# Sixty-four prompt tokens moved from a dense expert pass to a row-by-row one

## The chip, the cores and the metric

The kernel runs on one core of one Trainium2 chip. The metric is the device time of one launch in microseconds, as a median of runs. TensorE (PE) multiplies matrices, VectorE (DVE), ScalarE (ACT) and GpSimd (POOL) do the elementwise work, GpSimd also issues the indirect DMAs that gather rows, and SyncE (SP) issues all other DMAs.

## The reference

One transformer layer is computed for 1024 prompt tokens and for 32 sample tokens (8 sequences of 4). A projection feeds a state-space mixer and a windowed attention, both are joined by an output projection and a layer norm, and then comes a feed-forward part in which every token chooses 8 heads x 16 of 16384 experts. Only this last part is touched by the change:

```python
def block(xb):                      # xb: tokens x 1024, after the first layer norm
    qh = jnp.einsum('td,de->te', xb, w_q).reshape(-1, PEER_HEADS, PEER_DKEY)
    ...                             # top 16 of 128 keys on two sides, top 16 of their 256 sums
    e = ...                         # 128 expert numbers for each token
    g = jax.nn.softmax(sc.astype(F32), axis=-1)
    hid = jax.nn.gelu(jnp.einsum('thkd,td->thk', u_tab[e], xb).astype(F32), approximate=False)
    return jnp.einsum('thk,thkd->td', (g * hid).astype(xb.dtype), v_tab[e])
```

The result goes through `layer_norm(ALPHA * h + peer_ffn(h, ...))`. The tables `u_tab` and `v_tab` hold 16384 rows of 1024 floats (64 MB each).

## The kernel before, in words

**Two parts.** `PARTS` cuts the prompt into tokens 0 to 511, which go with the 32 sample tokens, and tokens 512 to 1023. `part(0)` and `part(1)` run `first` (projections, attention), `second` (scan, gates) and `third` (output projection, first norm), and `route` scores the keys and takes the top 16s on VectorE. Matrices are multiplied in three products of rounded parts (`hh`/`hl`, `whi`/`wlo`): each weight block `wraw` of 256 KB comes by a DMA of SP, ScalarE rounds it to `whi` (L366), and GpSimd or VectorE takes the rest `wlo` (L367). One weight block of 1024 x 128 is a step: 8 x 3 matmuls for each piece of its token columns, all at L425.

**Two ways through the experts.** The first way goes row by row (`gathers`). For 128 tokens at a time and for each of their 128 choices, one indirect DMA (L1823) fetches 128 rows of `u`, 512 KB, and VectorE multiplies and sums them against the token (L1849); then the same with 128 rows of `v`, which VectorE adds with weights (L1854). That is one row step for each (table, choice). The second way is dense (`dense`): for a set of tokens every one of the 16384 experts is computed, `gelu(u x)` times a table `g` that holds the token's gate or zero, and then `v` times that. There are 16 chunks of 1024 experts; a chunk is 8 steps over `u` (`hidden`) and 8 steps over `v` (`output`), 256 steps in all.

**Who goes which way.** `EXTRA = 64` splits the first part: tokens 0 to 447 (`TG`) go by row, tokens 448 to 511 are dense. The row plan has three tiles of 128 tokens with 2 x 128 row steps each, and a tile of 64 tokens whose choices are folded in two halves over the 128 partitions (`halfe`, `halfg`), with 2 x 64 row steps: 896 row steps. Dense are the 512 tokens of the second part, the 64 and the 32 sample tokens: `TE` = 608 columns, in the pieces `TPC` of 320 and 288.

**What sets the order.** The program is written out by generators ("lanes"). A step of matmuls is cut into ticks; at each tick the lanes advance by their rate, and what they emit stands there in every engine's queue. The row steps are such a lane, `pumping`. It starts in part 1 once `chooses` has the first tile's experts, at the rates `GATHER`, stands still at the end of `third`, runs at 0.2 per tick while the dense tables are made, and in the main loop at

```python
self.pumping.rate = self.left / ((len(steps) - 8) * DTICKS - 20)
```

so that what is left of the plan is spread over the 248 steps behind the first 8, with `DTICKS` = 4 ticks each. `ROWS` = 6 row buffers and `LOOK` = 5 mean that a row is fetched five row steps ahead, and a fetch waits until VectorE has used the buffer's last row. All queues are in order: on GpSimd the fetches stand between the casts `wlo`, on VectorE the row steps stand between `weigh` (L1671), `low` (L1677) and the sums of `output` (L1695).

**The tables.** Before the main loop `gates` makes the dense table in groups of 4 tokens: VectorE compares (`oo`, L1602), GpSimd weighs (L1604), TensorE multiplies (L1611), ScalarE stores to `gst` (L1621), and 32 tokens at a time go to DRAM (`gd`, 2 MB). The groups come in the order sample tokens, then the 64, then the four tiles of part 1: 152 groups. For the first two the experts were chosen earlier (`given = 2`); for the four tiles `choose` runs between the groups. Six steps over `u` run meanwhile, with `EARLY` ticks. The main loop reads the table back as `g`, 2.5 MB for each chunk.

Of the kernel before, what the change touches and what calls it, by code (L numbers as in the profile page):

```python
# [19 lines left out]
NB = 8  # L20
# [60 lines left out]
TICKS, ETICKS = [[6, 4, 4, 4], [5, 4, 4, 4]], 6  # L81
GATHER = [2.5, 3.2, 3, 0.0, 0.2]
DTICKS = 4
CACHE, SAMPLE, TOPS, TOPS2, CHOOSE = 0.1, 1.4, 1, 0.6, 1

START, LO1, LO2, LO3, LO4, LO5 = "vp", ["vvp", "vpp"], ["vp", "vp"], ["vp", "vp"], ["p", "p"], "vpppppp"
# [51 lines left out]
def layout(inp):  # L138
# [62 lines left out]
    "y": (TG, D),  # L201
# [12 lines left out]
def unlayout(r):  # L214
    y = r["y"]
    y1 = r["y1"].transpose(2, 1, 0).reshape(TE, D)
    yp = np.concatenate([y, y1[PD:PD + EXTRA], y1[:PD]])
# [6 lines left out]
    def cache(old, new):  # L224
# [3 lines left out]
        yp[None], y1[PD + EXTRA:].reshape(NB, NL, D),  # L228
# [23 lines left out]
class Build:  # L252
# [40 lines left out]
    def run(self):  # L293
# [16 lines left out]
        self.half_e = cp.tile([128, 64], I32, name="halfe")  # L310
        self.half_g = cp.tile([128, 64], F32, name="halfg")
# [3 lines left out]
        self.hx = dpool.tile([128, 8, NX], F32, name="hx")  # L315
# [3 lines left out]
        self.pumping, self.seat = None, None  # L319
# [9 lines left out]
    def start(self):  # L329
# [157 lines left out]
    def part(self, hf):  # L487
# [9 lines left out]
        if self.smp:  # L497
            xp = self.open("smp", side="right")
# [10 lines left out]
    def first(self, hf):  # L509
        two = len(self.pcs) == 2  # L510
        self.ring = [0, 1, 2] if two else [0, 1]
        self.ms, self.pvz = (4, 5) if two else (2, 3)
        self.sc = [self.bank(6), self.bank(7)] if two else [self.bank(4, 2), self.bank(6, 2)]
# [80 lines left out]
    def keyrows(self, ap, pr, ps):  # L594
# [11 lines left out]
        if not self.last:  # L606
            nc.sync.dma_start(self.kd[self.hf][:, pr], kk[:, :PT])
        if self.smp:
            nc.gpsimd.tensor_copy(self.sample[1][:, pr], kk[:, PT:])
        self.ready[pr] += 1  # L610

    def values(self, ap, pr, ps):
# [11 lines left out]
        for a in range(0, len(self.tiles), 4):  # L624
            tl = self.tiles[a:a + 4]
# [482 lines left out]
    def gated(self, zp, ps, k):  # L1108
# [23 lines left out]
        if k % 3 == 2:  # L1132
            yield

            while k < 11 and self.at < 3:
# [14 lines left out]
    def third(self, hf):  # L1150
# [82 lines left out]
        for i, (s, n) in enumerate(cuts):  # L1233
            for j, (k, h) in enumerate(END):
                self.step(self.parted(self.h), [acc[k][i]], [(s, n)], ETICKS, False, True, order=[4, 5, 6, 7, 0, 1, 2, 3], q=q0 + j,
# [11 lines left out]
        for i, (s, n) in enumerate(cuts):  # L1247
            while norms[i].live:
                norms[i].run()
            self.step(self.x, [out[i] if np_ == 2 else out[0][:, s:s + n]], [(s, n)], 4, q=q0, ahead=i == 0)  # L1250
        self.close(f"z{hf}", f"y{hf}", f"att{hf}", f"x{hf}")
        if not self.last:
# [3 lines left out]
            nc.sync.dma_start(self.hx, self.r[:, :, self.PT - EXTRA:])  # L1256
        else:
            sp = self.open(f"n{hf}", side="right")
            hx = sp.tile([128, 8, NX], F32, name="hx", tag="hx", bufs=1)
# [90 lines left out]
    def route(self, hf, first):  # L1350
# [10 lines left out]
        self.routed = self.tiles[:n], self.best  # L1361
        if self.last:
            others = [self.lane(self.experts(sp, *v)) for v in zip(((self.smp_e, self.smp_g), (self.ecol[-1], self.gate[-1])), (NS, 128), self.given)]
        else:
            self.gp = self.open("g")
# [533 lines left out]
```

## Time and profile before

| what | value |
|---|---|
| median of 3 runs | 3781.95 us (3780.59 to 3783.11) |
| the profiled execution's own time | 3779.82 us |
| its span, first to last instruction | 3778.1 us |
| mean granted TensorE clock | 0.959 |
| busy share of the span: PE, DVE, POOL, ACT | 92%, 71%, 63%, 34% |
| moved by DMA | 875.33 MB, mean 232 GB/s |

Spans below are in microseconds from the first instruction. The stages are: both parts up to 1760, the tables from 1760 to 2050, a turn into the main loop to 2090, the main loop to 3738, and the last norm. The granted clock is given as a share of full speed (1.00 is 2.4 GHz). The DMA share is the mean busy share of the core's 16 DMA engines; q0 carries the gathered rows, q1 everything that SP issues. A matmul's duration overlaps the next one's, so its cost is read from the distance of starts.

### The profile page before, as it was taken

The page shows a single profiled execution, that of the slowest core. Times are in us where ns is not written, and L with a number is a line of the kernel's source. Part 1 is how long each engine was busy: PE and PEld are TensorE (multiplying, and loading weights), DVE is VectorE, ACT ScalarE, POOL GpSimd, SP SyncE. Part 2 cuts the span into 40 slices and gives each one's busy share as a digit, 9 for nine tenths or more (in the row PEclk, how much of TensorE's full clock was granted, in tenths as well). Part 3 has the DMA queues.
Part 4 walks back from the last instruction along what each step waited for, and adds up shares of the span by engine and source line. Part 5 has one row for each costly group of instructions (what it writes and reads, how often), then busy time and mean ns, then how long its engine had stood idle before and what let it go on. Part 6 is the DMA issues. An engine that isn't in the chain of part 4 may idle for free.

```text
span 3778.1 us, 61732 instructions
## 1 busy us (share of the span) xinstructions
PE 3475.6 (92%) x22691; PEld 3142.5 (83%) x22691; DVE 2684.3 (71%) x5449; ACT 1285.9 (34%) x2347; POOL 2370.2 (63%) x2235
## 2 busy tenths in 40 slices
PE   8999998997998787996778999999999999999998
PEld 7757777986666565775668999999999999999997
DVE  2335655379768988889998967677767667776775
ACT  3423224252443334242556222222232222223222
POOL 3303555344656678734787877777778777777774
PEclk9999999998999898987898999999999999999999
DMA  5352235752446557811557889999999999999993
GB/s 166 116 164 85 84 103 182 252 178 79 141 141 226 169 161 235 300 58 65 186 196 283 319 317 355 329 322 313 325 319 365 327 329 334 319 315 322 327 328 132
DMA packets 386959, 875.33 MB, mean 232 GB/s; under 512 B 40416, under 2 KB 151392, under 8 KB 383712
## 3 DMA queue, kind: packets, MB, share of 16 engines
q0 software_dynamic: 129024, 469.82, 34.9%
q1 hardware_dynamic: 257632, 401.57, 32.0%
q8 instruction: 178, 2.92, 0.3%
q14 instruction: 125, 1.02, 0.1%
HBM read 805.34 MB, written 94.65 MB: 238 GB/s over the span
## 4 chain that ended last, share of the span: by engine, by line
PE 45%; DVE 8%; issue 4%; POOL 3%; DMA 2%; ACT 1%; DVEq 0%; POOLq 0%; SPq 0%; ACTq 0%
PE P L425 38%; PE P L1745 5%; DVE oo L1602 2%; POOL oo L1604 1%; DMA row<-in_v,ecol 1%; PE P L1611 1%; DVE P L1854 1%; POOL row L1823 1%; POOL wlo L367 1%; DVE mr L1341 0%; POOL eq L1542 0%; PE P L1275 0%; DMA lng<-in_ln 0%; DVE keys L1345 0%; DVE keys L1339 0%
## 5 line engine op out<-in xcount | busy, mean ns | idle before, releaser
L367 POOL TENSOR_TENSOR wlo<-wraw,whi 128x512 fp32r<-128x512 f32 (+1 forms) x621 | 807.0, 1305 | 604.0 <-ACT whi L366 548.7
L366 ACT ACTIVATE whi<-wraw 128x512 fp32r<-128x512 f32 (+1 forms) x820 | 499.9, 625 | 1390.8 <-PE P L425 583.0
L425 PE MATMUL P<-hh,whi 128*128 128x320 f32 (+3 forms) x2648 | 654.6, 312 | 7.5 <-ACT hh L1304 4.6
L425 PE MATMUL P<-hl,whi 128*128 128x320 f32 (+3 forms) x2648 | 653.6, 311 | 3.5 <-POOL hl L1296 3.2
L425 PE MATMUL P<-hh,wlo 128*128 128x320 f32 (+3 forms) x2648 | 647.7, 310 | 4.8 <-POOL wlo L367 4.5
L1854 DVE SCALAR_TENSOR_TENSOR P<-row,hid,P 128x1024 f32<-128x1024 f32 x448 | 575.3, 1284 | 28.7 <-DMA row<-in_v,ecol 14.7
L1849 DVE SCALAR_TENSOR_TENSOR row<-row,P 128x1024 f32<-128x1024 f32 x403 | 478.4, 1213 | 62.8 <-DMA row<-in_u,ecol 25.9
L1823 POOL DMA_INDIRECT row<-in_u,ecol x384 | 389.1, 1013 | 155.4 <-DVE row L1849 79.4
L425 PE MATMUL P<-xh,whi 128*128 128x272 f32 (+4 forms) x1288 | 434.6, 347 | 37.2 <-ACT xh L366 15.7
L425 PEld LDWEIGHTS P<-hh,whi 128*128 128x128 f32 x2648 | 445.2, 191 | 17.5 <-ACT hh L1304 5.0
L425 PEld LDWEIGHTS P<-hl,whi 128*128 128x128 f32 x2648 | 445.2, 191 | 13.1 <-POOL hl L1296 4.7
L425 PEld LDWEIGHTS P<-hh,wlo 128*128 128x128 f32 x2648 | 444.8, 191 | 13.1 <-POOL wlo L367 4.7
L1823 POOL DMA_INDIRECT row<-in_v,ecol x384 | 378.7, 986 | 101.7 <-issue 49.2
L425 PE MATMUL P<-xl,whi 128*128 128x272 f32 (+4 forms) x1288 | 421.9, 338 | 7.8 <-POOL xl L367 6.1
L425 PE MATMUL P<-xh,wlo 128*128 128x272 f32 (+4 forms) x1288 | 418.2, 335 | 0.0
L367 DVE TENSOR_TENSOR wlo<-wraw,whi 128x512 fp32r<-128x512 f32 (+1 forms) x199 | 212.6, 1069 | 211.1 <-ACT whi L366 202.3
L425 PE MATMUL P<-ah,wlo 128*128 128x320 f32 (+1 forms) x1536 | 341.3, 301 | 4.5 <-POOL wlo L367 4.5
L425 PE MATMUL P<-ah,whi 128*128 128x320 f32 (+1 forms) x1536 | 342.1, 302 | 0.0
L425 PE MATMUL P<-al,whi 128*128 128x320 f32 (+1 forms) x1536 | 340.8, 301 | 0.0
L425 PEld LDWEIGHTS P<-xh,whi 128*128 128x128 f32 (+1 forms) x1288 | 247.8, 196 | 69.8 <-ACT xh L366 17.0
L425 PEld LDWEIGHTS P<-xl,whi 128*128 128x128 f32 (+1 forms) x1288 | 247.6, 196 | 35.0 <-POOL xl L367 8.2
L425 PEld LDWEIGHTS P<-xh,wlo 128*128 128x128 f32 (+1 forms) x1288 | 247.2, 196 | 25.4 <-issue 4.2
(386 smaller groups left out, 6147.9 us busy)
## 6 DMA issues: line engine op xcount, KB each, us to landing
wraw<-in_ut SPq DMA_DIRECT2D x256, 256.0 KB, 6.0
wraw<-in_vd SPq DMA_DIRECT2D x256, 256.0 KB, 4.8
wraw<-in_wt SPq DMA_DIRECT2D x176, 256.0 KB, 2.9
gd<-gst SPq DMA_DIRECT2D x19, 2048.0 KB, 7.3
g<-gd SPq DMA_DIRECT2D x90, 320.0 KB, 9.8
wraw<-in_wo SPq DMA_DIRECT2D x64, 256.0 KB, 3.8
wraw<-in_wq SPq DMA_DIRECT2D x64, 256.0 KB, 3.0
out_sk<-in_ck SPq DMA_DIRECT2D x8, 2040.0 KB, 10.9
```

Of the source, the lines that this page charges most:

```text
L366: nc.scalar.activation(hi, src, AF.Copy)
L367: (eng or nc.vector).tensor_tensor(lo, src, hi.bitcast(F32), op=ALU.subtract)
L425: nc.tensor.matmul(outs[i], w[a][:, k, :m], x[b][k][:, s:s + n], start=first and st, stop=last and sp)
L1602: nc.vector.tensor_tensor(oo, iota.unsqueeze(1).unsqueeze(1).to_broadcast([128, 2, 4, 128]), eT[:, 0:2, t0:t0 + 4].unsqueeze(3).to_broadca ...
L1604: nc.gpsimd.tensor_tensor(oo[:, 1], oo[:, 1], eT[:, 2, t0:t0 + 4].unsqueeze(2).to_broadcast([128, 4, 128]), op=ALU.mult)
L1611: nc.tensor.matmul(gp[:, k * 128:(k + 1) * 128], oo[:, 1, k], oo[:, 0, k], start=True, stop=True)
L1745: nc.tensor.matmul(outs[i][j], self.ws[q0 + i][wi][:, e, :], x[xi][e][:, s:s + m], start=e == p == 0, stop=e == last and p == 2)
L1823: nc.gpsimd.indirect_dma_start(out=rows[k], out_offset=None, in_=t["uv"[tab]], in_offset=bass.IndirectOffsetOnAxis(ap=tables(gi)[0][:, s:s ...
L1849: nc.vector.scalar_tensor_tensor(r, r, 1.0, at, op0=ALU.mult, op1=ALU.mult, accum_out=hid[:, s:s + 1])
L1854: nc.vector.scalar_tensor_tensor(at, r, hid[:, s:s + 1], at, op0=ALU.mult, op1=ALU.add)
```

## The change

`EXTRA`, `TG`, `NX`, `halfe` and `halfg` go. All 512 tokens of the first part go by row: four tiles of 128, 4 x 2 x 128 = 1024 row steps. Dense are the 512 tokens of part 1 and the 32 samples: `TE` = 544 columns, `TPC` = 288 and 256, 17 table blocks of 32 tokens where there were 19, 136 groups where there were 152. `given` becomes 1, and while the tables' first tile has its experts chosen, the lane first waits for the top 16s of part 1 to be finished. `fetch` now asks whether a tile's experts are chosen (`self.chosen`). Several constants become lists by part with the same values for these two parts (`GATHER`, `TICKS`, `ETICKS`, `TOPS`, `SCORES`), and some conditions are written for more than two parts; those leave these two parts' instructions as they were. Rates of the row lane in part 1 and beside the tables are the same, so the same number of row steps is done before the main loop, and what is added falls into it.

```diff
 PARTS = [(0, 512, True), (512, 512, False)]
-EXTRA = 64
 TD, PD = PARTS[-1][:2]
-TG = TD - EXTRA
-NX = EXTRA + NS
-TE = PD + NX
+TE = PD + NS
...
-GATHER = [2.5, 3.2, 3, 0.0, 0.2]
+GATHER, GATHERT = [[0, 0, 0, 0], [2.5, 3.2, 3, 0.0]], 0.2
...
 def chooses
-            if s + m > TG:
-                for src, dst in ((e, self.half_e), (g, self.half_g)):
-                    for k in range(2):
-                        self.nc.sync.dma_start(dst[64 * k:64 * k + 64], src[:64, 64 * k:64 * k + 64])
-            if i == 0:
+            self.chosen += 1
+            if not self.pumping:
                 self.pumping = self.lane(self.gen, self.rate)
...
 def gates
-        work = [(NS, PD + EXTRA, 0), (EXTRA, PD, 128 - EXTRA)] + [(m, s, 0) for s, m in tiles]
-        given = 2
+        work = [(NS, PD)] + list((m, s) for s, m in tiles)
+        given = 1
...
-            if t0 == work[w][2] and 0 < w < len(work) - 1:
+            if t0 == 0 and w < len(work) - 1:
                 gen = experts(w + 1)
             next(gen, 0)
-            if t0 == work[w][2] + work[w][0] - 4 * OBUFS:
+            if t0 == work[w][0] - 4 * OBUFS:
+                while w < given and self.top.live:
+                    yield
                 for _ in gen:
                     pass
...
 def gathers
-        plan = [(gi, tab, s) for gi in range(NTG) for tab in range(2) for s in range(min(128, TG - gi * 128))]
-        self.left = len(plan)
+        plan = [(gi, tab, k) for gi in range(NTG) for tab in range(2) for k in range(128)]
+        self.left, ahead = len(plan), [0]
...
-                if s == m - 1:
+                if s == 127:
                     acc = seat(gp.tile([128, D], F32, name="acc", tag="acc"), at) if moved else at
-                    if m < 128:
-                        up = gp.tile([128, D], F32, name="up", tag="gh")
-                        nc.sync.dma_start(up[:m], acc[m:])
-                        nc.vector.tensor_tensor(acc[:m], acc[:m], up[:m], op=ALU.add)
-                    self.norm2(acc[:m], t["y"][gi * 128:gi * 128 + m], m)
+                    self.norm2(acc, t["y"][gi * 128:gi * 128 + 128], 128)
```

On TensorE, from the first dense step on, a product of one `k` stands in two pieces. Before:

```order
L425 MATMUL P<-hh,whi 128x320
L425 MATMUL P<-hh,whi 128x288
L425 MATMUL P<-hl,whi 128x320
L425 MATMUL P<-hl,whi 128x288
L425 MATMUL P<-hh,wlo 128x320
L425 MATMUL P<-hh,wlo 128x288
```

Now:

```order
L423 MATMUL P<-hh,whi 128x288
L423 MATMUL P<-hh,whi 128x256
L423 MATMUL P<-hl,whi 128x288
L423 MATMUL P<-hl,whi 128x256
L423 MATMUL P<-hh,wlo 128x288
L423 MATMUL P<-hh,wlo 128x256
```

Both pieces are narrower by 32 columns; the number of matmuls of a step stays 48.

On GpSimd, in the main loop where two `v` steps run as one double step, row fetches (DMA `row`) stand between casts (`wlo`). Before:

```order
L367 TENSOR_TENSOR wlo_20898<-wraw_20753,whi_20897 128x512
L1823 DMA row_20921<-in_u,ecol1_75 128x1024
L367 TENSOR_TENSOR wlo_20898<-wraw_20789,whi_20897 128x512
L1823 DMA row_20953<-in_u,ecol1_75 128x1024
L1823 DMA row_20968<-in_u,ecol1_75 128x1024
L1823 DMA row_20995<-in_u,ecol1_75 128x1024
L1823 DMA row_21010<-in_u,ecol1_75 128x1024
L367 TENSOR_TENSOR wlo_21019<-wraw_20826,whi_21018 128x512
```

Now:

```order
L365 TENSOR_TENSOR wlo_19669<-wraw_19521,whi_19668 128x512
L1821 DMA row_19692<-in_u,ecol1_75 128x1024
L365 TENSOR_TENSOR wlo_19669<-wraw_19557,whi_19668 128x512
L1821 DMA row_19712<-in_u,ecol1_75 128x1024
L1821 DMA row_19727<-in_u,ecol1_75 128x1024
L1821 DMA row_19754<-in_u,ecol1_75 128x1024
L1821 DMA row_19769<-in_u,ecol1_75 128x1024
L1821 DMA row_19784<-in_u,ecol1_75 128x1024
L365 TENSOR_TENSOR wlo_19793<-wraw_19597,whi_19792 128x512
```

Five fetches stand in a row where four stood: the row lane's rate is higher, and the casts are as many as before.

On VectorE, in the tables, the choice of the first tile's experts (`eq`, `ef`, `ei`) stood between compares of groups (`oo`) and row steps. Before:

```order
L1540 TENSOR_TENSOR eq_15670<-sf_15634,cf_15633 128x1024
L1602 TENSOR_TENSOR oo_15672<-P_64,eT1_13982 128x1024
L1854 SCALAR_TENSOR_TENSOR P_64<-row_13641,hid_9238,P_64 128x1024
L1602 TENSOR_TENSOR oo_15687<-P_64,eT1_13982 128x1024
L1602 TENSOR_TENSOR oo_15698<-P_64,eT1_13982 128x1024
L1545 TENSOR_REDUCE ef_15669<-eq_15670 128x64
L1602 TENSOR_TENSOR oo_15710<-P_64,eT1_13982 128x1024
L1540 TENSOR_TENSOR eq_15721<-sf_15634,cf_15633 128x1024
L1602 TENSOR_TENSOR oo_15723<-P_64,eT1_13982 128x1024
```

Now:

```order
L1542 TENSOR_TENSOR eq_15574<-sf_15566,cf_15565 128x1024
L1547 TENSOR_REDUCE ef_15573<-eq_15574 128x64
L1542 TENSOR_TENSOR eq_15578<-sf_15566,cf_15565 128x1024
L1547 TENSOR_REDUCE ef_15573<-eq_15578 128x64
L1549 CAST ei_15563<-ef_15573 128x128
L1558 TENSOR_SCALAR ej_15584<-ei_15563 128x128
L1559 TENSOR_SCALAR ej_15584<-ei_15563 128x128
L1561 CAST en_15585<-ej_15584 128x256
L1604 TENSOR_TENSOR oo_15593<-P_64,eT_13975 128x1024
```

Nothing stands between its steps any more: the compares that stood there are those of the 64 tokens, which are gone, and the row step there comes later.

## Rows read from the trace of the kernel before

**Rows 1.** Busy time by stage; columns in the second line, last two DMA share and rate.

```profile
core 0: us, PE busy (x) PEld busy (x) DVE busy (x) ACT busy (x) POOL busy (x), PEclk, DMA share, GB/s
0.00:1760.00 1760.00, 1557.40 (x9145) 1248.29 (x9145) 1177.19 (x3529) 634.23 (x1373) 885.99 (x888) 0.94 0.47 154
1760.00:2050.00 290.00, 221.01 (x1503) 205.18 (x1504) 275.11 (x389) 172.00 (x176) 229.12 (x213) 0.88 0.54 196
2050.00:2090.00 40.00, 32.00 (x204) 29.80 (x204) 24.52 (x23) 12.71 (x21) 20.85 (x17) 0.91 0.75 242
2090.00:3738.00 1648.00, 1638.99 (x11715) 1638.26 (x11714) 1186.25 (x1477) 453.18 (x753) 1230.21 (x1117) 1.00 0.92 324
3738.00:3778.00 40.00, 26.20 (x130) 20.99 (x128) 21.28 (x35) 13.81 (x26) 4.01 (x3) 0.83 0.18 63
```

**Rows 2.** What TensorE waited for in the main loop: us, times, longest.

```profile
PE P L425 <- POOL wlo L367: 9.0, 3, 4.5
```

**Rows 3.** TensorE's timeline in the main loop: start us, us, pieces of 320 and 288 columns.

```profile
2500.22 0.44 PE L425 MATMUL P<-hh,wlo 128*128 128x320 f32 x2
...
2502.74 0.44 PE L425 MATMUL P<-hh,wlo 128*128 128x320 f32 x2
```

**Rows 4.** TensorE's timeline in the first part's projections: 272 columns each.

```profile
158.34 0.29 PE L425 MATMUL P<-xh,whi 128*128 128x272 f32 x1
...
160.10 0.29 PE L425 MATMUL P<-xh,wlo 128*128 128x272 f32 x1
```

**Rows 5.** The DMA queues and issues of the main loop, 2090 to 3738 us.

```profile
DMA packets 245605, 534.47 MB, mean 324 GB/s; under 512 B 20965, under 2 KB 93413, under 8 KB 245462
q0 software_dynamic: 99040, 360.62, 60.3%
q1 hardware_dynamic: 146422, 171.91, 31.7%
g<-gd SPq DMA_DIRECT2D x90, 320.0 KB, 9.8
g<-gd SPq DMA_DIRECT2D x29, 256.0 KB, 8.6
```

**Rows 6.** Queues over 100 us of the main loop, with its row gathers.

```profile
q0 software_dynamic: 6066, 22.08, 62.0%
q1 hardware_dynamic: 9277, 10.28, 31.1%
row<-in_v,ecol POOLq DMA_INDIRECT x42, 6.6
```

**Rows 7.** Four short stretches, columns as in the first group.

```profile
1480.00:1500.00 20.00, 10.63 (x31) 7.36 (x30) 19.44 (x18) 8.62 (x17) 17.16 (x15) 0.69 0.86 291
1540.00:1580.00 40.00, 38.31 (x196) 32.17 (x196) 35.51 (x33) 9.13 (x15) 35.10 (x32) 1.00 0.99 377
2500.00:2600.00 100.00, 100.00 (x718) 100.00 (x717) 71.53 (x71) 27.12 (x46) 73.57 (x68) 1.00 0.94 325
2645.00:2685.00 40.00, 40.00 (x288) 40.00 (x288) 27.56 (x27) 9.62 (x16) 29.61 (x29) 1.00 1.01 367
```

**Rows 8.** GpSimd's groups in 1200 us of the main loop: count | busy, mean ns | idle before.

```profile
L367 POOL TENSOR_TENSOR wlo<-wraw,whi 128x512 fp32r<-128x512 f32 x308 | 398.4, 1299 | 148.1 <-ACT whi L366 129.6 <-issue 16.2
L1823 POOL DMA_INDIRECT row<-in_v,ecol x256 | 247.0, 965 | 72.1 <-issue 35.6 <-DVE P L1854 17.3 <-PE P L425 2.9
```

**Rows 9.** VectorE's two row steps in the same 1200 us.

```profile
L1854 DVE SCALAR_TENSOR_TENSOR P<-row,hid,P 128x1024 f32<-128x1024 f32 x256 | 328.9, 1285 | 14.3 <-DMA row<-in_v,ecol 8.8 <-ACT P L1827 1.3
L1849 DVE SCALAR_TENSOR_TENSOR row<-row,P 128x1024 f32<-128x1024 f32 x256 | 303.8, 1214 | 45.0 <-DMA row<-in_u,ecol 25.9 <-issue 10.8 <-POOL wlo L367 7.8
```

**Rows 10.** Two groups of the table stage, 1760 to 2050 us.

```profile
L1602 DVE TENSOR_TENSOR oo<-P,eT 128x1024 f32<-128x1024 f32 x152 | 178.3, 1213 | 8.0 <-PE P L1611 3.0 <-ACT eT L1565 2.8 <-PE P L1563 2.1
L1542 POOL TENSOR_TENSOR eq<-eq,cf 128x1024 f32<-128x1024 f32 x8 | 18.9, 2365 | 0.0
```

More of the change, by code (lines that the diff above doesn't have):

```diff
@@ L1249, in third @@
                 norms[i].run()
-            self.step(self.x, [out[i] if np_ == 2 else out[0][:, s:s + n]], [(s, n)], 4, q=q0, ahead=i == 0)
+            self.step(self.x, [out[i] if np_ == 2 else out[0][:, s:s + n]], [(s, n)], TICKS[hf][3], q=q0, ahead=i == 0)
         self.close(f"z{hf}", f"y{hf}", f"att{hf}", f"x{hf}")
@@ L1360, in route @@
         self.turns = LO4[hf]
-        self.routed = self.tiles[:n], self.best
+        self.routed = self.tiles[:n], self.best, self.sbest if self.smp else None
+        held = SCORES[hf]
         if self.last:
-            others = [self.lane(self.experts(sp, *v)) for v in zip(((self.smp_e, self.smp_g), (self.ecol[-1], self.gate[-1])), (NS, 128), self.given)]
+            others = [self.lane(self.experts(sp, (self.smp_e, self.smp_g), NS, self.given))]
         else:
-            self.gp = self.open("g")
+            if not hf:
+                self.gp = self.open("g")
             self.xrp = sp
@@ L1411, in tops @@
             if with_smp:
-                yield from self.pairs(pr, skeys, self.sbest, 0)
+                yield from self.pairs(pr, skeys, sbest, 0)
         if with_smp:
+            sbest = self.sbest
             skeys = [pr.tile([128, 1, 2, 2, TK], d, name=f"skeys{i}", tag=f"skeys{i}", bufs=1) for i, d in enumerate((F32, U32))]
         self.pays = nc.gpsimd
-        top = self.lane(tops(), TOPS)
+        top = self.lane(tops(), TOPS[hf])
         self.fins.append(Lane(score(0, first), 1))
         for ct in range(1, 16):
-            self.wait(lambda: ct - past[0] <= 2)
+            self.wait(lambda: ct - past[0] <= held)
             self.proj(TICKS[self.hf][3], lambda ps, ct=ct: score(ct, ps))
@@ L1434, in pairs_room @@
         if self.last:
-            self.given = [pool.tile([128, 3, 128], F32, name=f"eT{i}") for i in range(2)]
+            self.given = pool.tile([128, 3, 128], F32, name="eT")
         return [pool.tile([128, n, PH, TK], d, name=f"best{i}") for i, d in enumerate((F32, U32, F32))]
@@ L1616, in store @@
             w, t0 = groups[q]
-            at = work[w][1] + t0 - work[w][2]
+            at = work[w][1] + t0
             if at % 32 == 0:
@@ L1828, in seat @@
             return dst
-        for k in range(LOOK):
-            fetch(k)
+        fetch(LOOK - 1)
         for k, (gi, tab, s) in enumerate(plan):
-            m = min(128, TG - gi * 128)
+            while ahead[0] <= k:
+                fetch(k)
+                yield
             hs = heads[gi]
```

133 lines of the change are left out of this document (66 added, 67 removed).

## The prediction

> **What bounds the kernel now.** I read the stages first [rows 1]. The main loop is 1648 us of 3778, and there TensorE is busy 1639 us at a granted clock of 1.00; it waits 9.0 us in all, three times [rows 2]. So the main loop goes at TensorE's pace. Beside it the DMA engines are busy 0.92 of the time, GpSimd 1230 us (75%), VectorE 1186 us (72%) [rows 1]. The reader should see that TensorE is the bound by a margin of 8% only: the next resource is the DMA engines, and the change loads just them.
>
> In the table stage VectorE is busy 275 of 290 us and TensorE 221 at a clock of 0.88 [rows 1]: there VectorE is the bound. The 1760 us before it hold both parts' projections, attention and scans. Nothing of the change stands there but a few small copies (the folded tables of the 64 tokens, 96 columns of `hx` that become 32), so I leave them at zero.
>
> The pace of a step: 100 us of the main loop hold 718 matmuls [rows 7], a step has 48, so a step takes 6.685 us, and 1648 us are 246.5 steps. The timeline says the same: from 2500.22 to 2502.74 stand 9 pairs of pieces, 0.280 us each [rows 3], and 24 pairs are 6.72.
>
> **TensorE's share of the change.** A pair is now 288 + 256 = 544 columns. The first part's projections have just these 544 columns, as 2 x 272: 14 distances from 158.34 to 160.10 are 0.1257 us each [rows 4]. 48 of them are 6.03 us. If TensorE stays the bound, the main loop gains (6.685 - 6.03) x 246.5 = 161 us. This is the gain that the change can have at most.
>
> **The DMA engines' share.** The row plan grows from 896 to 1024 row steps, and all 128 more fall into the main loop, since the lane's rates before it are unchanged. A row step moves 22.08 MB / 42 = 0.526 MB [rows 6]; the main loop's 360.62 MB [rows 5] are 686 of them, so it will hold 814, 3.30 for each step. SP's queue moved 171.91 MB [rows 5], of which the table `g` is 90 x 320 KB + 29 x 256 KB = 37.1 MB, which falls by 2 of 19 blocks, 3.9 MB. A step then moves 3.30 x 0.526 + (171.9 - 3.9) / 246.5 = 1.736 + 0.682 = 2.42 MB. At 6.03 us that would be 401 GB/s, where the main loop has 324 [rows 1]. So what the engines can do at most decides. Two stretches show them full: 2645 to 2685, inside the main loop with the table's small packets among the rest, 367 GB/s at a share of 1.01, and 1540 to 1580, rows and weights only, 377 GB/s at 0.99 [rows 7]. By these a step takes 2.42 / 0.377 = 6.42 us to 2.42 / 0.367 = 6.59 us. The mix of the new main loop, with less of the table than the first stretch and some of it, lies between; I take 6.50. The main loop then gains (6.685 - 6.50) x 246.5 = 46 us, from 64 to 23 by the two rows.
>
> The Trainium skill, HBM Reference, section Specifications, gives about 358 GB/s for a core, half of what a stack shared by two cores has; its section Access says that a core that streams alone measures well above that, about 425. The trace agrees with neither as a ceiling for this mix: 377 GB/s is more than the one, and no stretch read here comes to the other. By the first a step would take 6.75 us and the main loop would lose 16 us; by the second it would take 5.7 us and TensorE would stay the bound.
>
> **GpSimd and VectorE.** In 1200 us GpSimd casts 308 times at 1.299 us, 1.72 for each step, and issues each row in 0.965 us with 35.6 / 256 = 0.14 us of its own issue time before it [rows 8]. A new step needs 3.30 x 1.105 + 1.72 x 1.299 = 5.88 us of it: below 6.50, but 90%. It waits 148.1 / 308 = 0.48 us before a cast, nearly always for ScalarE's half of it [rows 8]. I count most of that as waiting that goes once GpSimd is late rather than early; if none goes, its step is 5.88 + 1.72 x 0.48 = 6.71 us. VectorE gets 128 more steps of 1.285 or 1.214 us [rows 9], 160 us, and its other work narrows by a tenth: (1186 + 160) / (246.5 x 6.50) = 84%. It has room, but it is in order: a late row holds up the sums that TensorE's banks wait for.
>
> **The tables.** 16 of 152 groups go. VectorE needs 1.213 us for one [rows 10], 19 us in all, and a group's share of the stage is 290 / 152 = 1.91 us, 30 us in all. Against it the first tile's choice, which stood between the compares of the 64 tokens, now stands alone on VectorE: its compare, GpSimd's multiplication of 2.365 us [rows 10] and its sum, twice, follow each other with nothing between, so some 5 us of VectorE lie idle in the multiplications alone and about as much again in the round trips around them. I take -14 us, between -30 and 0. The turn into the main loop and the last norm, 40 us each [rows 1], have a tenth fewer columns in half of their work: -5 us, between -8 and 0. The fourth tile's `norm2` replaces that of the 64 tokens with its fold: nothing.
>
> **Sum.** -46 - 14 - 5 = -65 us on the profiled execution's 3779.8 us, 3715. The median stands 2.1 us above that execution, so 3717.
>
> **Rivals.**
> *TensorE stays the bound.* The full stretches may not be the ceiling: a queue that always has fetches waiting may do better than one that is full for 40 us. Then the step is 6.03 us: -161 - 19 = -180, 3602 us. For it: TensorE kept its pace through both full stretches (288 matmuls in 40 us are 0.139 us each, as elsewhere [rows 7]). Against it: 401 GB/s would have to be held for 1500 us.
>
> *No gain in the main loop.* GpSimd's in-order queue keeps its waits: a cast waits for ScalarE, which waits for TensorE to free a weight buffer, and the fetches behind the cast wait with it, so the DMA engines run empty just when they are needed. Step 6.71 us: +6 - 19 = -13, 3769 us, with partial cases from 3740 to 3790. For it: 0.48 us before each cast now; the double steps bunch casts. Against it: six row buffers keep up to five fetches, 2.6 MB or 7 us of transfer, waiting in the queues.
>
> *The DMA engines are slower under this load.* If a row keeps costing the engine time that it has on average now, 62.0 us for 42 rows, 1.476 us, and SP's queue 31.1 us for 14.96 steps, 2.08 us [rows 6], a step needs 3.30 x 1.476 + 2.08 x 0.682 / 0.697 = 6.91 us of fully busy engines: +55 - 19 = +36, 3818 us; at today's share of 0.94 [rows 7] it would be 7.35 us, 3927. It decides for slower as soon as the full engines move less than 2.42 / (6.685 + 19 / 246.5) = 358 GB/s over the whole loop. For it: the mean over 100 us is 325 GB/s at 0.94, that is 346 for a full share. Against it: both full stretches move 367 and more, so a packet's time shrinks when the next one is waiting. By the Trainium skill, HBM Reference, section Specifications, whose 358 GB/s stands above, the time would come out at no change, within this rival and the one before it; the two full stretches speak against that figure as a ceiling.
>
> *It does not do what it says.* The order of instructions shows the narrower pieces, the added fetches and nothing else that counts, so I give this nothing.
>
> **How the numbers follow.** Forecast, a step of 6.2 to 6.6 us, 3665 to 3740 us: 0.51. TensorE's pace or near it, below 3665: 0.14. No gain in the main loop, 3740 to 3790: 0.21. Slower by the engines, above 3790: 0.14. A measurement of this kernel can tell 0.2%, 7.6 us, from no change. Faster than 3774 are the first two and two thirds of the third: 0.79. Within 0.2%: 0.08. Slower than 3790: 0.13. For 8 in 10 the range leaves out half of the fast case and most of the slow one: 3640 to 3800.
>
> **What would show it.** In the profile of the changed kernel the main loop should be near 1600 us, with the DMA share at 0.97 or more, 365 to 380 GB/s, and TensorE busy about 93% with waits of `wlo` or of VectorE's sums in its line; 288-column pieces at the same distance per column; a clock near 1.00, since at 96% busy it was 1.00 and at 53% it was 0.69 [rows 7]. GpSimd's share should be near 90% and its wait before a cast clearly below 0.48 us. The table stage should be 270 to 285 us. The forecast is wrong upwards if DMA stays below 358 GB/s, or if TensorE's waits let the clock fall; and wrong downwards if the share stays below 0.95 with TensorE still at 100%.

## The result, and the profile after

| | before | after |
|---|---|---|
| median, us | 3781.88 (3780.59 to 3783.11) | 3760.33 (3757.49 to 3761.98) |
| profiled execution: time, span | 3779.82, 3778.1 | 3761.2, 3759.4 |
| moved by DMA | 875.33 MB | 933.74 MB |

The ratio is 0.9942, 95% interval 0.9925 to 0.9959: faster by 21.5 us, a third of the 65 that were forecast, inside the range. The stages of the changed kernel, with the columns and in the order of [rows 1]:

```profile
core 0: us, PE busy (x) PEld busy (x) DVE busy (x) ACT busy (x) POOL busy (x), PEclk, DMA share, GB/s
0.00:1756.00 1756.00, 1552.75 (x9142) 1245.35 (x9142) 1172.26 (x3527) 632.89 (x1372) 883.89 (x888) 0.94 0.47 154
1756.00:2018.00 262.00, 186.03 (x1336) 174.28 (x1337) 243.33 (x368) 150.43 (x155) 204.70 (x191) 0.86 0.52 193
2018.00:2046.00 28.00, 18.16 (x144) 17.68 (x142) 12.06 (x11) 8.21 (x12) 14.10 (x13) 0.89 0.96 320
2046.00:3722.00 1676.00, 1542.21 (x11806) 1516.70 (x11807) 1341.62 (x1683) 450.60 (x765) 1365.48 (x1254) 0.97 0.98 358
3722.00:3759.00 37.00, 23.67 (x136) 19.42 (x135) 19.81 (x35) 12.83 (x26) 3.39 (x3) 0.87 0.18 61
```

TensorE has 97 us less work in the main loop (1542 against 1639 in [rows 1]) and the loop is no shorter. To compare kernels I need the same stretch in each. The double steps, where two `v` steps run as one (L1745, now L1749), give it: their group in the timeline of TensorE names the first and the last start, which lie 242 steps apart (15 chunks of 16 steps and the last double step). First the kernel before, then after; durations are least/median/most in ns:

```profile
L1745 PE MATMUL P<-ah,whi x512: 293/306/636, 2070.4 to 3707.0; 128*128 128x320 f32 x86, 128*128 128x288 f32 x85
```

```profile
L1749 PE MATMUL P<-ah,whi x512: 278/292/609, 2046.2 to 3688.2; 128*128 128x288 f32 x86, 128*128 128x256 f32 x85
```

So the span's 18.7 us are -24.2 up to the first double step, +5.4 over the **242 steps** (1636.6 to 1642.0, 6.763 to 6.785 us a step), and 0.1 behind them. The gain came ahead of the main loop, in the tables. The main loop, from which 46 us were to come, gave none.

Two quiet stretches and two others of the main loop after the change show what it is made of:

```profile
2300.00:2400.00 100.00, 95.19 (x749) 94.07 (x748) 77.81 (x130) 26.57 (x46) 82.87 (x77) 1.00 1.01 370
2500.00:2600.00 100.00, 94.11 (x730) 93.12 (x729) 84.86 (x81) 27.40 (x48) 83.94 (x78) 0.98 1.01 370
2600.00:2700.00 100.00, 85.74 (x641) 84.34 (x641) 74.78 (x83) 26.72 (x43) 77.80 (x71) 0.93 0.96 356
3100.00:3200.00 100.00, 85.49 (x652) 83.70 (x652) 79.68 (x81) 28.35 (x46) 73.72 (x68) 0.95 0.96 351
```

In the quiet ones 48 matmuls take 6.4 to 6.6 us, near the 6.50 that I took, at a full DMA share. In the others some 90 matmuls, 12 us, are missing. In each of these a tile of 128 row tokens ends (I call that a tile change) and its last norm, `norm2`, stands in the queues. The one at 2673 us, in pieces of 5 us:

```profile
2675.00:2680.00 5.00, 4.75 (x39) 4.53 (x37) 3.33 (x7) 4.22 (x6) 0.00 (x0) 1.00 1.00 391
2680.00:2685.00 5.00, 0.77 (x4) 0.55 (x4) 5.00 (x9) 2.17 (x4) 4.39 (x2) 0.97 0.06 22
2685.00:2690.00 5.00, 0.68 (x3) 0.68 (x4) 1.52 (x2) 1.14 (x2) 4.37 (x5) 0.50 0.68 222
2690.00:2695.00 5.00, 5.00 (x24) 5.00 (x24) 3.09 (x5) 1.14 (x2) 4.21 (x5) 0.50 1.00 365
2695.00:2700.00 5.00, 5.00 (x42) 5.00 (x42) 3.56 (x6) 0.42 (x1) 4.21 (x5) 1.00 1.02 367
```

The chain is to be read from three timelines. GpSimd (start us, us, and in brackets its idle time before and what ended it):

```profile
2672.54 0.95 POOL L1821 DMA_INDIRECT row<-in_u,ecol  x1 [0.16 <-issue]
2680.53 4.80 POOL L1873 TENSOR_TENSOR acc<-acc,lng 128x1024 f32<-128x1024 f32 x2 [7.04 <-DMA lng<-in_ln]
2685.48 1.26 POOL L1821 DMA_INDIRECT row<-in_u,ecol  x1
```

SP's queue in the same stretch:

```profile
2672.91 0.96 SPq L1872 DMA_DIRECT2D lng<-in_ln  x2
2685.36 0.34 SPq L1874 DMA_DIRECT2D out_y<-acc  x1
2689.30 7.68 SPq L391 DMA_DIRECT2D wraw<-in_vd  x4
```

TensorE:

```profile
2682.49 0.41 PE L423 MATMUL P<-hl,whi 128*128 128x288 f32 x2
2689.32 0.82 PE L423 MATMUL P<-hh,wlo 128*128 128x288 f32 x2 [6.42 <-POOL wlo L365]
```

`norm2` loads gamma and beta (`lng`, 0.5 MB each) through the row buffers. These loads are issued while the engines still move queued rows (391 GB/s), GpSimd waits 7.0 us for them, then multiplies and adds for 4.8 us, and for 12 us it issues no row and casts no weight. The DMA engines run empty (22 GB/s), TensorE waits for `wlo`, and then starts at half clock. SP's `out_y` waits for GpSimd too; the weight load behind it comes 4 us later, when GpSimd's next cast has ended, so a delay by `out_y` itself is not shown.

Before the change GpSimd stood no shorter at the tile changes. Its group from 2150 to 3450 us (count | busy, mean ns | idle before), before and after:

```profile
L1879 POOL TENSOR_TENSOR acc<-acc,lng 128x1024 f32<-128x1024 f32 x6 | 14.4, 2399 | 28.5 <-DMA lng<-in_ln 28.3
```

```profile
L1873 POOL TENSOR_TENSOR acc<-acc,lng 128x1024 f32<-128x1024 f32 x6 | 14.1, 2356 | 24.1 <-DMA lng<-in_ln 17.3 <-DVE P L1675 6.6
```

These are three tile changes; the fourth one's `norm2` starts on GpSimd at 3709 us (before: 3724), behind the 242 steps. Yet before the change TensorE waited for `wlo` only 9.0 us in the whole main loop [rows 2].

### The profile page after: what moved, and what is told of

Same layout as the page of the kernel before. It is cut to its first block, busy times and chain, and to the rows that moved or that the text cites. A ratio compares the mean times of both kernels' runs of the same rounds, so it can differ in the third digit from the quotient of the medians.

```text
span 3759.4 us, 61914 instructions
## 1 busy us (share of the span) xinstructions
PE 3322.8 (88%) x22560; PEld 2973.4 (79%) x22560; DVE 2789.1 (74%) x5620; ACT 1255.0 (33%) x2329; POOL 2471.6 (66%) x2347
## 2 busy tenths in 40 slices
DMA packets 396689, 933.74 MB, mean 248 GB/s; under 512 B 42080, under 2 KB 144992, under 8 KB 393696
## 5 line engine op out<-in xcount | busy, mean ns | idle before, releaser
L1852 DVE SCALAR_TENSOR_TENSOR P<-row,hid,P 128x1024 f32<-128x1024 f32 x512 | 658.3, 1286 | 125.5 <-DMA row<-in_v,ecol 109.5
L423 PE MATMUL P<-hh,whi 128*128 128x288 f32 (+3 forms) x2648 | 633.6, 305 | 45.9 <-DVE al L1681 36.6
L423 PE MATMUL P<-hh,wlo 128*128 128x288 f32 (+3 forms) x2648 | 624.4, 301 | 26.9 <-POOL wlo L365 26.2
L1821 POOL DMA_INDIRECT row<-in_u,ecol x512 | 511.4, 999 | 187.4 <-DVE row L1847 90.8
L423 PE MATMUL P<-hl,whi 128*128 128x288 f32 (+3 forms) x2648 | 626.8, 302 | 3.8 <-POOL hl L1295 2.5
L1821 POOL DMA_INDIRECT row<-in_v,ecol x512 | 502.4, 981 | 128.2 <-issue 76.8
L423 PE MATMUL P<-ah,whi 128*128 128x288 f32 (+1 forms) x1536 | 326.7, 293 | 31.7 <-DVE r L1699 25.9
L423 PE MATMUL P<-ah,wlo 128*128 128x288 f32 (+1 forms) x1536 | 324.7, 291 | 5.4 <-POOL wlo L365 5.4
L423 PE MATMUL P<-al,whi 128*128 128x288 f32 (+1 forms) x1536 | 324.0, 291 | 0.0
L423 PEld LDWEIGHTS P<-ah,whi 128*128 128x128 f32 x1536 | 240.3, 192 | 34.8 <-issue 19.2
```

Of the source, the lines that this page charges most:

```text
L423: nc.tensor.matmul(outs[i], w[a][:, k, :m], x[b][k][:, s:s + n], start=first and st, stop=last and sp)
L1821: nc.gpsimd.indirect_dma_start(out=rows[k0], out_offset=None, in_=t["uv"[tab]], in_offset=bass.IndirectOffsetOnAxis(ap=self.ecol[gi][:, s: ...
L1852: nc.vector.scalar_tensor_tensor(at, r, hid[:, s:s + 1], at, op0=ALU.mult, op1=ALU.add)
```

## The experiments

Each kernel was timed against the kernel before in the same session (whose medians there lay between 3776 and 3779 us). The table gathers them; "242 steps" is the time of the group above in that kernel's timeline, GB/s and DMA share are those from 2150 to 3450 us. The 242 steps are read from one profiled execution of each kernel, and the executions of a kernel differ by 3 to 18 us of the whole (e5's lie from 3792 to 3810, e2's from 3721 to 3736), so a difference of a few us says nothing.

| run | median us | ratio, interval | 242 steps, us | GB/s, share |
|---|---|---|---|---|
| kernel before | 3781.88 | 1 | 1636.6 | 327, 0.93 |
| kernel after | 3760.33 | 0.9942 (0.9925 to 0.9959) | 1642.0 | 363, 0.99 |
| e4_896_rows | 3597.89 | 0.9533 (0.9517 to 0.9548) | 1485.0 | 358, 0.99 |
| e5_before_1024_rows | 3804.75 | 1.0065 (1.0044 to 1.0086) | 1660.0 | 363, 1.00 |
| e6_before_norm_vector | 3764.83 | 0.9967 (0.9953 to 0.9981) | 1627.2 | 328, 0.94 |
| e13_before_1024_norm | 3775.31 | 0.9991 (0.9981 to 1.0000) | 1637.2 | 367, 1.01 |
| e1_resident_only | 3744.34 | 0.9912 (0.9896 to 0.9929) | 1627.4 | 364, 0.99 |
| e2_norm_vector | 3725.36 | 0.9873 (0.9852 to 0.9895) | 1609.8 | 369, 1.01 |
| e3_half_rows | 3676.98 | 0.9740 (0.9724 to 0.9756) | 1566.7 | 245, 0.79 |
| e8_half_rows_norm_vector | 3654.06 | 0.9666 (0.9645 to 0.9686) | 1544.2 | 247, 0.79 |
| e9_half_rows_relieved | 3603.02 | 0.9538 (0.9522 to 0.9554) | 1496.5 | 255, 0.81 |
| e7_gpsimd_relieved | 3747.20 | 0.9922 (0.9905 to 0.9938) | 1623.2 | 369, 1.00 |
| e11_norm_vector_relieved | 3720.55 | 0.9848 (0.9830 to 0.9866) | 1609.1 | 369, 1.00 |
| e12_rows_early_relieved | 3699.45 | 0.9794 (0.9778 to 0.9811) | 1559.5 | 370, 1.01 |

**The change's two halves.** The narrower columns alone, on the changed kernel:

```diff
-        plan = [(gi, tab, k) for gi in range(NTG) for tab in range(2) for k in range(128)]
+        plan = [(gi, tab, k) for gi in range(NTG) for tab in range(2) for k in range(128 if gi < NTG - 1 else 64)]
...
```

> The changed kernel with the fourth tile's row steps cut from 128 to 64 for each table, so 896 row steps as before the change, and 544 dense tokens (64 of the 128 choices of the last 128 row tokens are left out). It is the change's TensorE half alone. Theory A: 694 row steps and 168 MB more in the main loop are 533 MB, 1441 us at 370 GB/s, so TensorE sets the pace at 6.03 us a step, 1487 us plus what is left of the stops: main loop 1490-1545 us, whole 3575-3630 us. A rival, narrower pieces don't pay for themselves because TensorE then waits for VectorE's sums or GpSimd's casts: main loop 1580-1640 us, whole 3665-3725 us.

The added rows alone, on the kernel before:

```diff
-        plan = [(gi, tab, s) for gi in range(NTG) for tab in range(2) for s in range(min(128, TG - gi * 128))]
+        plan = [(gi, tab, s) for gi in range(NTG) for tab in range(2) for s in range(128)]
...
-                                         in_offset=bass.IndirectOffsetOnAxis(ap=tables(gi)[0][:, s:s + 1], axis=0))
+                                         in_offset=bass.IndirectOffsetOnAxis(ap=tables(gi)[0][:, s % m:s % m + 1], axis=0))
...
```

> The kernel before with 128 row steps more: its last 64 tokens go through their choices twice, 1024 row steps in all, 608 dense columns (the row sums of these 64 tokens are doubled). It is the change's other half, the added rows alone. Theory A: about 605 MB in a TensorE-bound 1667 us are 363 GB/s, nearly what full engines move, and the four tile changes now stop TensorE: main loop 1680-1720 us, whole 3795-3835 us. Theory B, GpSimd's queue sets 6.71 us a step: whole 3785-3795 us. If the engines had the room that the prediction gave them and the stops stayed hidden: 3780-3785 us.

Both fell into the range of theory A. Over the 242 steps the columns alone give 152 us and the rows alone cost 23, yet together they cost 5: the halves don't add. (The profiled execution of e5 is the slowest of its four; by the medians the added rows cost 28 us of the whole.) e4 is the full gain of narrower columns; a quiet stretch of it:

```profile
2500.00:2600.00 100.00, 100.00 (x800) 100.00 (x800) 82.71 (x79) 27.88 (x48) 83.48 (x78) 1.00 1.00 366
```

48 of 800 matmuls are 6.00 us a step, the 6.03 that the first part's projections had promised. And the DMA share is 1.00 at 366 GB/s there too, while TensorE is never idle: a full share does not tell that the engines are late.

**The tile change.** In e2 gamma and beta are loaded once, behind the first two table loads, and VectorE does GpSimd's work:

```diff
-        nc.vector.tensor_scalar(acc, acc, mv[:m, 0:1], mv[:m, 1:2], op0=ALU.subtract, op1=ALU.mult)
-        for i, op in enumerate((ALU.mult, ALU.add)):
-            gb = gp.tile([128, D], F32, name="lng", tag="row", bufs=ROWS)
-            nc.sync.dma_start(gb[:m], self.t["ln2"][i:i + 1, :].to_broadcast([m, D]))
-            nc.gpsimd.tensor_tensor(acc, acc, gb[:m], op=op)
+        nc.vector.scalar_tensor_tensor(acc, acc, mv[:m, 0:1], self.lng[0], op0=ALU.subtract, op1=ALU.mult)
+        nc.vector.scalar_tensor_tensor(acc, acc, mv[:m, 1:2], self.lng[1], op0=ALU.mult, op1=ALU.add)
...
                 dp = self.open("dn", 2)
                 for i in range(2):
                     table(0, i)
+                self.lng = [dp.tile([128, D], F32, name=f"lng{i}", tag=f"lng{i}", bufs=1) for i in range(2)]
+                for i in range(2):
+                    nc.sync.dma_start(self.lng[i], t["ln2"][i:i + 1, :].to_broadcast([128, D]))
```

> The changed kernel, with norm2's gamma and beta fetched once ahead of the main loop into two tiles of their own (they came by two 0.5 MB loads through the row buffers at each of the four tile changes), and its multiplication and addition folded into two VectorE instructions (GpSimd had two of 2.4 us). Theory A, the four tile changes stop fetches, weight casts and then TensorE, and between them the DMA engines set the pace: the stops of some 10 to 15 us each go, and 4 MB less are moved, so the main loop falls from 1676 to 1610-1635 us and the whole to 3695-3725 us. Theory B, GpSimd's in-order queue sets the pace throughout: only its 4 x 4.8 us of work go, 3735-3750 us. Theory C, the engines were full through the tile changes too, taken over the loop: -11 us for the 4 MB, 3745-3755 us.

32 us less over the 242 steps, the whole at the upper edge of theory A. At the tile change the engines no longer run empty, though TensorE still loses some us there (VectorE has 5 us of `norm2` in its queue, and the rows and sums behind it are late):

```profile
2675.00:2680.00 5.00, 2.08 (x17) 1.86 (x15) 4.96 (x8) 3.84 (x6) 3.54 (x3) 1.00 0.91 345
2680.00:2685.00 5.00, 4.73 (x25) 4.73 (x26) 5.00 (x10) 1.85 (x5) 3.82 (x4) 0.66 0.81 261
```

e1 keeps GpSimd's two instructions and only makes the tiles resident:

```diff
         for i, op in enumerate((ALU.mult, ALU.add)):
-            gb = gp.tile([128, D], F32, name="lng", tag="row", bufs=ROWS)
-            nc.sync.dma_start(gb[:m], self.t["ln2"][i:i + 1, :].to_broadcast([m, D]))
-            nc.gpsimd.tensor_tensor(acc, acc, gb[:m], op=op)
+            nc.gpsimd.tensor_tensor(acc, acc, self.lng[i], op=op)
...
```

> The changed kernel with gamma and beta resident as in e2_norm_vector, but GpSimd still multiplies and adds (2 x 2.4 us at each tile change). It parts the wait for the loads from GpSimd's work. At the tile change at 2673 us GpSimd stood 7.0 us for the load and then worked 4.8 us, with no fetch issued in 13 us. e2 took 32 us off the 242 steps. If the load is what stops GpSimd (and 4 MB fewer bytes): 1615-1625 us of the 1642, whole 3730-3745 us. If GpSimd's own 4 x 4.8 us matter as much: 1625-1635 us, whole 3742-3752 us.

14.6 us of the 32 are the wait for the loads with their bytes, 17.6 GpSimd's own instructions, which last 3 x 4.8 = 14.4 us at the three tile changes: the second case. The control has e2's edit on the kernel before:

> The kernel before with the same edit of norm2 as in e2_norm_vector (gamma and beta resident, two VectorE instructions in place of GpSimd's). A control. Theory A: before the change TensorE lost 9.0 us in all over the loop, since the engines and queues had slack to hide the tile changes, so at most 9 us can be had there, and a few more in the last norm2 at the end: whole 3765-3780 us, ratio 0.996 to 1.000. A rival, the edit is simply better everywhere (less work on GpSimd, 4 MB less): 3740-3755 us as in the changed kernel, where it took 35 us off.

There it is worth 9.4 us over the 242 steps. GpSimd stood as long before the change, and it cost a third. The likely reason is that TensorE's pace left the queues room to make up for it; e5, which fills that room, and the next run bear on this.

**Rows on top of that, wide columns.** e13 is e5's edit with e2's.

> e5_before_1024_rows (608 dense columns, 1024 row steps, the last 64 tokens' row sums doubled) with norm2 as in e2_norm_vector. From the first double step to the last the kernel before took 1637 us, with the new norm2 1627, with 128 row steps more 1660. If the 23 us of e5 are the tile changes alone: 1630-1640 us, whole 3770-3785 us. If the bytes already limit it (some 600 MB in 1640 us are 366 GB/s, where full engines move 368 to 371): 1645-1655 us, whole 3785-3797 us.

The first case: 1637.2, so with the new `norm2` 128 more row steps cost 10 us under 608 columns, and 23 with the old one (1660.0 in e5 against 1636.6). But its row shows how near the edge that is:

```profile
2150.00:3550.00 1400.00, 1393.85 (x9957) 1393.03 (x9956) 1142.02 (x1476) 388.68 (x641) 1138.56 (x1057) 1.00 1.01 367
```

TensorE is at 99.6% and the engines move 367 GB/s. e2, with the same rows and 10% fewer columns, moves 369. From e13 to e2 the loop gains 27 us, 2%, for 10% less TensorE work.

**Are bytes the limit?** e3 halves the bytes of each row fetch and keeps the number of instructions (VectorE reads the half twice, in lines that are not shown here):

```diff
-                nc.gpsimd.indirect_dma_start(out=rows[k0], out_offset=None, in_=t["uv"[tab]],
+                nc.gpsimd.indirect_dma_start(out=rows[k0][:, D // 2:], out_offset=None, in_=t["uv"[tab]].rearrange("e (a n) -> (e a) n", a=2),
...
```

> The changed kernel with half of each gathered row: every row fetch brings 2 KB for each token and not 4 KB, from the same number of fetches, and VectorE reads the half twice, so GpSimd's and VectorE's instructions stay (the sums over the row experts are not the reference's). Main loop 600 MB before, some 390 MB now. Theory A, the engines set the pace between the tile changes: TensorE takes over at 6.03 us a step, 1487 us, plus what is left of four stops, main loop 1490-1545 us, whole 3575-3630 us. Theory B, GpSimd's in-order queue or the issue of fetches sets it: no change beyond 10 us, 3745-3765 us.

Neither theory: 75 us less over the 242 steps, half of what theory A wanted, and theory B's "no change" is as wrong. Bytes held the loop, and something else stood right behind. e8 takes the tile changes out of e3 with e2's edit; e9 also gives VectorE a third of the casts:

```diff
-LO3, LO4, LO5 = ["vp", "vp"], ["p", "p"], "vpppppp"
+LO3, LO4, LO5 = ["vp", "vp"], ["p", "p"], "vpp"
```

> e3_half_rows and e2_norm_vector together: half of the rows' bytes (the row sums are not the reference's) and norm2 on VectorE. From the first double step to the last, 242 steps, e3 took 1567 us and 544 columns with 896 row steps took 1485. If the tile changes are what e3 still loses: 1500-1520 us, whole 3610-3630 us. If GpSimd's instructions set e3's pace (3.36 fetches at 0.95 + 0.25 us and 1.72 casts at 1.30 us are 6.27 us a step, 1517 us for 242 steps, with the stops on top): 1530-1550 us, whole 3640-3660 us.

> e8_half_rows_norm_vector with one weight cast in three on VectorE: neither bytes, nor tile changes, nor GpSimd (5.8 us a step) should hold TensorE. If these three are all there is: TensorE's 6.01 us a step, 1455-1490 us for the 242 steps, whole 3565-3600 us. If VectorE's in-order queue is a limit of its own (it gets 0.27 us a step more): no better than e8, or worse.

e8 came out by its second case, GpSimd. Its groups there, 2150 to 3450 us (203.5 steps; columns as in [rows 8]):

```profile
L365 POOL TENSOR_TENSOR wlo<-wraw,whi 128x512 fp32r<-128x512 f32 x349 | 453.6, 1304 | 11.5 <-issue 4.5 <-ACT whi L364 1.3
L1824 POOL DMA_INDIRECT row<-in_u,ecol x384 | 375.2, 977 | 91.1 <-issue 78.3 <-DVE row L1852 7.2 <-DMA row<-in_u,ecol 1.7
L1824 POOL DMA_INDIRECT row<-in_v,ecol x305 | 296.9, 973 | 72.8 <-issue 65.9 <-DVE P L1857 3.1 <-DVE r L1699 1.4
```

GpSimd hardly waits for anybody (0.03 us before a cast), and is still occupied all the time: of the 163.9 us before its 689 fetches, 0.24 each, the view names 144.2 as its own issue time. That is 6.39 us a step. Relieved of 0.5 us (e9), the loop is at 6.18 us a step, 1% above e4, a few us over the expected range. So bytes and tile changes held the changed kernel above TensorE's pace, and GpSimd stood right behind them.

**GpSimd alone.** e9's edit of the casts on the changed kernel, and on e2:

> The changed kernel with one weight cast in three on VectorE where it was one in seven: GpSimd has 1.33 casts a step and not 1.72, 0.5 us less of 6.5, and VectorE 0.27 us more. Theory A (the engines' bytes set the pace between the tile changes): same within 15 us, 3745-3770 us. Theory B (GpSimd sets it): up to 0.5 x 242 = 120 us less, 3640-3700 us. A third, VectorE's in-order queue already delays TensorE: slower, 3770-3800 us.

> e2_norm_vector with one weight cast in three on VectorE as in e7_gpsimd_relieved. In e2 the engines move 365-376 GB/s at a share of 1.00 or more nearly throughout, so bytes should be all that is left: 596 MB at 371 GB/s are 6.55 us a step, 1585-1605 us for the 242 steps (e2: 1610), whole 3700-3720 us. If GpSimd still costs what e7 took off the changed kernel (19 us) on top: 1585-1595 us, whole 3695-3708 us. If VectorE's in-order queue, now 5 us longer at each tile change and 0.27 us a step, is next: no better than e2, 3720-3735 us.

e7: 19 us over the 242 steps, 13 of the whole by the medians and 8 by the ratios, whose intervals overlap: theory A. Once `norm2` is off GpSimd, the relief gives 0.7 us over the 242 steps (1609.8 to 1609.1) and 5 by the medians, not to be told from nothing; e11 lies above its first range and by time alone would pass for the third case. The rates speak for bytes: e2, e7, e11 and e12 move 369 to 370 GB/s at full share, with GpSimd busy 76 to 82% and VectorE 82 to 85%; e9, with half the bytes, had VectorE 94% busy and went faster. A relieved GpSimd seems to help to make up for a stop more than between stops; more than that these runs don't show. Whether more row buffers would let the queues make up for a stop was not tried.

**A version that beats both.** e12 is e11 with more row steps in the second part, before the loop:

```diff
-GATHER, GATHERT = [[0, 0, 0, 0], [2.5, 3.2, 3, 0.0]], 0.2
+GATHER, GATHERT = [[0, 0, 0, 0], [4.5, 3.2, 3, 0.0]], 0.2
```

> e11_norm_vector_relieved with the first rate of the row lane in the second part raised from 2.5 to 4.5 row steps a projection, where the DMA engines are at 0.4 to 0.5 and TensorE at 96-100%: some 40 row steps (21 MB) leave the main loop. If bytes set the loop's pace: 21 MB at 371 GB/s are 57 us, the 242 steps 1530-1555 us; the second part may lengthen by up to 40 x 1.25 us if VectorE has no room there: whole 3640-3700 us, most likely near 3660. If the loop is bound by something else now: 3690-3720 us.

It is 2.1% faster than the kernel before, the upper edge of what was expected; the 242 steps, 1559.5 us, lie just above their range. Of some 40 row steps 36 moved: up to the first double step there are 243 fetches, in e11 207. Over the 242 steps the `u` fetches are 384 in both; those of `v`, in e11 and then in e12:

```profile
L1824 POOL DMA_INDIRECT row<-in_v,ecol x429: 935/942/1483, 2060.5 to 3654.6; - x143
```

```profile
L1824 POOL DMA_INDIRECT row<-in_v,ecol x395: 932/940/1464, 2093.2 to 3638.8; - x198
```

The loop lost 50 us, and 34 x 0.526 MB at 368 GB/s, its rate in both, are 49: the bytes account for it. VectorE had little room in the second part: the first table group came 33 us later than in e11, for 36 x 1.25 = 45 us of row steps.

## Why the prediction was right or wrong

**TensorE's floor: right.** 6.03 us a step was forecast, e4 has 6.00 in quiet stretches.

**The tables and the turn: right in sum.** Forecast -14 and -5; measured -24.2 up to the first double step and nothing behind the last. The stage between the first and last `oo` went from 285 to 260 us, -25, between my -14 and the 30 us of an even share (16 groups at 1.91 us), so I had probably put too much against the share for the first tile's lone choice. The first `oo` came 4 us earlier, and the turn grew by 5 us. None of this was looked into further.

**The main loop: the step that failed.** Forecast -46 us (-45 over the 242 steps), measured +5.4. Two terms of the sum were mis-sized, the first by more.

1. "The fourth tile's `norm2` replaces that of the 64 tokens with its fold: nothing." I asked what the new tile change costs more than the old one, and never what hides the three that stand inside the loop. TensorE's three waits of [rows 2], 9.0 us in all, were what showed of them. With the margin gone they hold the loop up: e2 takes 32 us off the changed kernel by an edit worth 9.4 before, 23 us of the 50 that were missed. (By the ratios of the whole it is 26 us against 12.) That is a least value, since e2 still dips at each tile change.

2. The step of 6.50 us. Between the tile changes it nearly held. Three stretches without one, of the changed kernel and then of e2, and one of the kernel before (columns as in [rows 1]):

```profile
2200.00:2600.00 400.00, 377.50 (x2926) 372.80 (x2925) 322.90 (x429) 108.23 (x188) 332.24 (x309) 0.99 1.01 369
2700.00:3100.00 400.00, 375.11 (x2911) 369.93 (x2910) 322.12 (x432) 105.79 (x182) 331.26 (x308) 0.99 1.01 369
3300.00:3600.00 300.00, 283.51 (x2190) 278.67 (x2189) 245.22 (x313) 81.17 (x140) 252.06 (x235) 0.99 1.00 370
```

```profile
2200.00:2600.00 400.00, 379.63 (x2942) 375.60 (x2941) 327.87 (x429) 108.83 (x189) 332.37 (x309) 0.98 1.01 371
2700.00:3100.00 400.00, 380.22 (x2933) 375.93 (x2932) 326.94 (x430) 106.40 (x182) 332.08 (x310) 0.98 1.01 371
3300.00:3600.00 300.00, 283.44 (x2192) 278.38 (x2191) 248.09 (x302) 80.55 (x140) 249.16 (x233) 0.99 1.01 370
```

```profile
2300.00:2700.00 400.00, 400.00 (x2866) 400.00 (x2866) 283.94 (x365) 105.40 (x178) 298.82 (x275) 1.00 0.94 329
```

48 matmuls take 6.58 us after the change, 6.55 in e2 and 6.70 before. At these paces 242 steps would take 1592, 1584 and 1621 us; the rest of the 242 steps, 50, 26 and 15 us, lies around the tile changes and at the ends. So the change took 29 us off between the tile changes (forecast 45) and put 35 on around them and at the ends (forecast 0): that is the +5.4. By this reading some 35 of the 50 us missed belong to the first term and 16 to the second.

A step moves 2.43 MB there (6.58 us at 369 GB/s), and 2.42 had been forecast. The fetches are 3.36 a step over the 242 steps where I had 3.30: I spread the rows evenly over 246.5 steps, but the lane is paced to end before the loop does. The two full stretches [rows 7] bounded the rate well (367 and 377); the sustained rate, 369 to 371, lies nearer the lower one.

The Trainium skill, HBM Reference, section Specifications (TRN2), has about 358 GB/s for a core and about 425 for one that streams alone (the prediction names another section for the second). The trace agrees with neither for this mix: 367 to 370 GB/s were held over 1300 us and more.

**GpSimd: the margin was misread.** I gave a step 5.88 us with 0.14 us of issue before a fetch; e8 shows 0.24 before a fetch, 0.21 of it named issue, and 6.39 us a step with GpSimd hardly waiting. [rows 8] had 72.1 / 256 = 0.28 us before a fetch already, of which I counted only the half named issue. GpSimd's 6.39 are 4% below e2's 6.65 (1609.8 us for 242 steps). That the wait before a cast would fall from 0.48 was right: in the changed kernel, 2150 to 3450 us, it is 52.2 us for 328 casts, 0.16:

```profile
L365 POOL TENSOR_TENSOR wlo<-wraw,whi 128x512 fp32r<-128x512 f32 x328 | 424.9, 1298 | 52.2 <-ACT whi L364 41.9 <-PE P L423 3.7 <-issue 1.3
```

**The signs I had named.** DMA share 0.97 or more: 0.98. TensorE about 93% busy: 92%. GpSimd's share near 90%: 81% busy, without its issue time. Tables 270 to 285 us: 262. Main loop near 1600 us: 1676. TensorE's longest waits in the changed kernel from 2150 to 3450 us (us, times, longest) are for VectorE's `al` and sums, which stand behind late rows (VectorE waited 136 us for rows of `u` there), and for `wlo`, the longest at a tile change:

```profile
PE P L423 <- DVE al L1681: 28.4, 20, 3.8
PE P L423 <- POOL wlo L365: 27.2, 15, 13.3
PE P L423 <- DVE r L1699: 21.8, 11, 3.5
```

The rate, 365 to 380 GB/s, holds in quiet stretches, and the loop's mean is 358. The granted clock is 0.97 and not 1.00; it is 0.93 and 0.95 in the two stretches with a tile change above and 0.98 to 1.00 in the quiet ones.

**The rivals.** The time is that of "no gain in the main loop" (3740 to 3790), and its picture of GpSimd's in-order queue with the fetches behind a waiting instruction was right. But the instruction was `norm2`'s and not a cast: the casts' waits fell. "The DMA engines are slower" was to decide below 358 GB/s over the whole loop; the loop's mean came out just there, from stops and not from slower packets. "TensorE stays the bound" holds only with 128 row steps fewer (e4). Two slips stand in the working: of the two full stretches only the one in the main loop has the 288 matmuls that were counted for this rival (the other has 196, of other widths, with TensorE 96% busy [rows 7]), and the range 3665 to 3740 us does not fit its steps of 6.2 to 6.6: by the sum 6.2 gives 3643.

## What to carry to other kernels

Before taking work off the engine that sets the pace, list the rare stops that its slack hides now (here loads that an in-order queue waits for, and 4.8 us of other work in it), and price each as if nothing hid it: the same `norm2` edit was worth 9 us with slack and 32 without. Where a second and a third resource stand within 10% of the first, halves of a change don't add (-152 and +23 made +5), so the sum has to be made for the slowest of all, with the rates held over the whole stage. Test them one by one and then together: only e9, which lifts all three, came within 1% of e4's pace.

## What the runs showed of the hardware

A busy DMA share of 1.00 says little of the room left. It stood at 0.99 to 1.01 from 358 GB/s (e4, TensorE at full pace) to 370 (e12, TensorE held). The engine time of one fetch (128 rows) is not fixed either: before it was 62.0 us for 42 fetches [rows 6], 1.48 us each at a share of 0.94; in the changed kernel 68.8% of 1300 us for 645, 1.39 us at 0.99; and with half the bytes (e3) 42.2% for 678, 0.81 us at 0.79, 58% and not half. Why is not shown. Their queue, from 2150 to 3450 us, after and in e3:

```profile
q0 software_dynamic: 92833, 338.04, 68.8%
```

```profile
q0 software_dynamic: 54156, 177.51, 42.2%
```

TensorE's clock adds to a stop: with no matmul from 2683 to 2689 us, the granted clock was 0.50 (1.2 GHz) from 2685 to 2695, and the first 5 us of full work held 24 matmuls where the next 5 held 42.
